# Splitting the two opening x loads of a mixture-of-experts kernel between two DMA issuers

## The chip, the cores and the metric

The kernel runs on one core of one Trainium2 chip. The metric is device time in microseconds (us), as the median of several runs. Before the change it is 181.49 us, the median of 3 runs that lie between 181.38 and 181.49.

## The reference

There are 8 experts. Each takes its own 256 tokens of 512 numbers through two matrix products with a ReLU between them. All data is float32 in the chip's main memory.

```python
n_experts, capacity, hidden, expert_hidden = 8, 256, 512, 2048
h = np.matmul(x, w1) + b1[:, np.newaxis, :]      # x [8,256,512], w1 [8,512,2048]
h = np.maximum(h, 0)
return np.matmul(h, w2) + b2[:, np.newaxis, :]   # w2 [8,2048,512]
```

The weights w1 and w2 are 4.2 MB each for each expert, 67 MB in all. They are used once, so the kernel is mostly a stream of loads.

## The kernel before, in words

The matrix products are done in float16. A DMA that GpSimd (POOL) issues changes float32 to float16 on its way, so w1 and w2 arrive in SBUF as float16, in `load_w1` (L84) and `load_w2` (L93). Each has three buffers. The x of experts 2 to 7 comes in the same manner, in two loads of several experts (`load_x`, L76). The x of the first two experts is the exception: it is loaded as float32 by SyncE (SP) at L190 into two tiles `x32`, each of 128 partitions with 2 token rows of 512 numbers (4096 bytes a partition, 512 KB a load), and VectorE (DVE) changes it to float16 at L201. The tiles come from `out_pool`, whose two buffers hold the results of experts 6 and 7 at the end.

Then x must be transposed, since TensorE (PE) contracts over partitions. DVE does this in 32x32 blocks: 16 instructions at L109 for each of the first two experts, 16 at L112 for each of the others. DVE also transposes the biases b1 into `b1T` with four instructions (L208).

`first_product(e)` runs 16 blocks of 4 matmuls (L121) into PSUM. After each block ScalarE (ACT) adds the bias, applies ReLU and writes float16 (L128). Its first activation therefore waits for `b1T`, and so does the activation-table load that stands ahead of it. `second_product(e)` runs 2 bias matmuls (L171) and 32 matmuls (L178); DVE and ACT copy the results out of PSUM (L156, L157). It trails the first product by `LAG = 3` experts.

Results of experts 0 to 3 and of 4 and 5 are gathered and stored by POOL (L140). Expert 6 is stored in three parts at L164: 25 rows by SP, 96 by ACT, 7 by SP. Expert 7 is stored by SP, in one part.

What sets the order: the instructions of PE and the DMAs of POOL are kept in program order by hand (`ordered`). The list `ring` says in which step each load is issued. A load into a weight buffer waits until the product that used it before is done. The other engines work through their own queues, in the order in which the program was written. In the opening, the program order is: the two x loads (SP), w1 of expert 0, b2, b1 rows (POOL), then the cast and transposes of expert 0, the cast and transposes of expert 1 (DVE; part of these come before and part after `b1T`), and the main loop, whose first step has w1 of expert 1, x of experts 2 and 3, and w1 of expert 2 on POOL.

The DMAs of SP go through one hardware queue (q1 in the profile), those of ACT through another (q10), and those of POOL through a software queue (q0). Before the change ACT issues one DMA in all, the 96 rows at L164.

Of the kernel before, what the change touches and what calls it, by code (L numbers as in the profile page):

```python
# [10 lines left out]
def kernel(  # L11
# [9 lines left out]
    nc = tc.nc  # L21
# [4 lines left out]
    P = 128  # L26
    nTB = T // P
# [54 lines left out]
    def load_w1(e):  # L82
        w1_sb[e] = w1_pool.tile([P, nKC, M], fp16, tag="w1", name="w1sb")
        ordered(nc.gpsimd.dma_start(  # L84
            out=w1_sb[e], in_=w1[e].rearrange("(p kc) m -> p kc m", kc=nKC)
        ))
# [100 lines left out]
    x32 = []  # L187
    for e in range(nXF32):
        x32.append(out_pool.tile([P, nTB, H], fp32, tag="out", name="x32"))
        nc.sync.dma_start(out=x32[e], in_=x[e].rearrange("(p tb) h -> p tb h", tb=nTB))  # L190
    load_w1(0)
    ordered(nc.gpsimd.dma_start(  # L192
        out=b2_sb,
        in_=b2.rearrange("e h -> (e h)").rearrange("(o f) -> o f", o=1),
# [12 lines left out]
    for b in range(nB):  # L207
        nc.vector.transpose(  # L208
            out=b1T[b * B : (b + 1) * B, nB - 1 - b : nB - 1 - b + nJ * B],
            in_=b1_rows.rearrange("r (i j) -> r j i", j=nJ),  # L210
# [55 lines left out]
```

## Time and profile before

| What | us |
|---|---|
| median of 3 runs | 181.49 |
| span of the profiled execution, first to last instruction | 179.7 |
| difference between the two | 1.8 |
| PE, DVE, ACT, POOL busy | 129.1, 88.0, 70.2, 13.1 |
| share of 16 DMA engines' span: q0, q1, q10 | 96.6%, 2.4%, 0.5% |
| read from and written to main memory | 71.39 MB, 4.19 MB |
| from issue to landing: the two x loads of L190 | 3.5 and 4.3 |
| granted TensorE clock, mean | 0.944 |

The profile is one execution, recorded by the hardware; the page does not give that execution's own whole time beside its span, so the runs' median stands there. Times in the views are counted from the first instruction. In a row of the timeline the first number is the start, the second the length, then engine, line, operation, what is written and read, and in brackets the idle time before it and what ended that. "SPq" and "ACTq" are rows of the issuing of a DMA; the transfer follows and is in the rows of the DMA queues. In the view of a stretch by slices, a digit is the busy share of the 16 DMA engines in tenths (9 is 90% or more).

### The profile page before, as it was taken

The numbers are of one execution on the slowest core, as the hardware profiler recorded it, in microseconds if no ns is written. First come the engines' busy times: TensorE is split into PE (matmuls) and PEld (weight loads), VectorE is DVE, ScalarE is ACT, GpSimd is POOL, SyncE is SP. The second block draws the span as 40 slices with busy tenths as digits, with TensorE's granted clock in tenths as the row PEclk, the third lists the DMA queues.
The fourth block names the chain that finished last, engine by engine and source line by source line (L and its number), as shares of the span: only waits on it lengthen the run. The fifth ranks groups of instructions, "written<-read, shape, count | busy, mean of one in ns | idle before, by whom it ended". The sixth has DMA issues, their size and how long they took to land.

```text
span 179.7 us, 1958 instructions
## 1 busy us (share of the span) xinstructions
PE 129.1 (72%) x784; PEld 85.8 (48%) x784; DVE 88.0 (49%) x125; ACT 70.2 (39%) x151; POOL 13.1 (7%) x28
## 2 busy tenths in 40 slices
PE   0005099969595970899969597969497887999950
PEld 0004079969592320795369244844195332433420
DVE  0999942987000199999999998003200020301010
ACT  0000459969593022483099005950586020020010
POOL 7000002120201010001010001000200021010000
PEclk9999999999998798589999889999999996999996
DMA  5999999999999999999999999999999999999996
GB/s 216 251 226 199 233 212 197 233 224 193 228 230 192 221 233 215 197 230 230 204 208 230 219 193 233 226 193 222 230 215 197 233 206 204 223 212 215 335 420 250
DMA packets 3829, 40.56 MB, mean 226 GB/s; under 512 B 461, under 2 KB 477, under 8 KB 1133
## 3 DMA queue, kind: packets, MB, share of 16 engines
q0 software_dynamic: 3232, 38.35, 96.6%
q1 hardware_dynamic: 476, 1.70, 2.4%
q10 hardware_dynamic: 112, 0.39, 0.5%
q8 instruction: 6, 0.10, 0.2%
q14 instruction: 3, 0.02, 0.0%
HBM read 71.39 MB, written 4.19 MB: 421 GB/s over the span
## 4 chain that ended last, share of the span: by engine, by line
DMA 66%; PE 26%; POOL 2%; another core or an unknown queue 1%; issue 1%; ACT 0%; POOLq 0%
DMA w1sb<-in_w_dram 44%; DMA w2sb<-in_w_dram 22%; PE po L178 18%; PE ph L121 8%; PE po L171 1%; POOL w1sb L84 1%; ACT out L157 0%; POOL x L76 0%; POOL b_sb L192 0%; POOL b_rows L196 0%; POOLq L250 0%
## 5 line engine op out<-in xcount | busy, mean ns | idle before, releaser
L121 PE MATMUL ph<-xT,w1sb 128*128 128x256 f16 x512 | 63.6, 289 | 34.8 <-DMA w1sb<-in_w_dram 23.9
L121 PEld LDWEIGHTS <-w1sb 128*128 128x128 f16 x512 | 59.0, 147 | 40.3 <-DMA w1sb<-in_w_dram 32.6
L178 PE MATMUL po<-w2sb,hT 128*128 128x512 f16 x256 | 61.4, 402 | 9.4 <-DMA w2sb<-in_w_dram 9.4
L112 DVE STREAM_TRANSPOSE xT<-x 32x256 f16<-32x256 f16 (+1 forms) x64 | 53.1, 889 | 25.6 <-DMA x<-in_x_dram 18.7
L128 ACT ACTIVATE hT<-ph,b1T 128x256 f16<-128x256 f32 x128 | 56.2, 474 | 13.6 <-PE ph L121 13.4
L178 PEld LDWEIGHTS <-hT 128*128 128x128 f16 x256 | 25.9, 102 | 44.7 <-issue 19.3
L156 DVE COPY out<-po 32x512 f32<-32x512 f32 (+2 forms) x22 | 15.1, 688 | 54.0 <-PE po L178 53.8
L157 ACT COPY out<-po 32x512 f32<-32x512 f32 (+2 forms) x22 | 12.7, 579 | 69.7 <-PE po L178 69.5
L109 DVE STREAM_TRANSPOSE xT<-x 32x256 f16<-32x256 f16 x32 | 14.0, 436 | 0.5
L93 POOL DMA_DIRECT2D w2sb<-in_w_dram x10 | 5.3, 534 | 72.8 <-PE po L178 72.8
L128 ACT ACT_TABLE_LOAD x1 | 1.3, 1283 | 20.5 <-DVE b1T L208 20.5
L84 POOL DMA_DIRECT2D w1sb<-in_w_dram x8 | 4.5, 558 | 63.2 <-PE ph L121 62.4
L171 PE MATMUL po<-b_sb,ones 1*128 1x512 f16 x16 | 4.8, 379 | 0.0
L208 DVE STREAM_TRANSPOSE b1T<-b_rows 32x512 f32<-32x512 f32 x4 | 4.1, 1035 | 0.1
L201 DVE CAST x<-x 128x1024 f16<-128x1024 f32 x2 | 1.5, 757 | 3.3 <-DMA x<-in_x_dram 3.3
L140 POOL DMA_DIRECT2D out_dram<-out x2 | 1.1, 542 | 10.9 <-ACT out L157 10.9
L171 PEld LDWEIGHTS <-ones 1*128 1x128 f16 x16 | 0.9, 92 | 2.1 <-issue 2.1
L76 POOL DMA_DIRECT2D x<-in_x_dram x2 | 1.1, 552 | 0.0
L197 DVE MEMSET ones<- 1x128 f16 x1 | 0.2, 165 | 0.8 <-PEq L250 0.8
L196 POOL DMA_DIRECT2D b_rows<-in_b_dram x1 | 0.5, 515 | 0.0
L192 POOL DMA_DIRECT2D b_sb<-in_b_dram x1 | 0.5, 513 | 0.0
L250 POOL MEMSET const-float32-0.0<- 128x1 f32 x1 | 0.1, 99 | 0.2 <-issue 0.2
(3 smaller groups left out, 0.3 us busy)
## 6 DMA issues: line engine op xcount, KB each, us to landing
w1sb<-in_w_dram POOLq DMA_DIRECT2D x8, 2048.0 KB, 34.5
w2sb<-in_w_dram POOLq DMA_DIRECT2D x6, 2048.0 KB, 46.8
w2sb<-in_w_dram POOLq DMA_DIRECT2D x4, 1024.0 KB, 24.0
out_dram<-out POOLq DMA_DIRECT2D x1, 2048.0 KB, 26.8
x<-in_x_dram SPq DMA_DIRECT2D x2, 512.0 KB, 3.9
x<-in_x_dram POOLq DMA_DIRECT2D x1, 1024.0 KB, 30.8
out_dram<-out POOLq DMA_DIRECT2D x1, 1024.0 KB, 17.8
x<-in_x_dram POOLq DMA_DIRECT2D x1, 512.0 KB, 24.0
```

The lines of the kernel that those rows point to most:

```text
L84: ordered(nc.gpsimd.dma_start(out=w1_sb[e], in_=w1[e].rearrange("(p kc) m -> p kc m", kc=nKC)))
L93: ordered(nc.gpsimd.dma_start(out=w2_sb[e][:, lo : lo + half], in_=src[:, lo : lo + half]))
L109: nc.vector.transpose(out=out[:, :, g, :, 0, :], in_=block[:, :, :, 0, :])
L112: nc.vector.transpose(out=out[:, tb, g], in_=block[:, tb])
L121: ordered(nc.tensor.matmul(out=ph, lhsT=w1_sb[e][:, kc, :].rearrange("p (q j) -> p q j", j=nJ)[:, :, j], rhs=xT[e][:, kc, :], start=(kc == 0),
L128: nc.scalar.activation(out=hT[e][:, j, :].rearrange("p (tb k i) -> p tb k i", tb=nTB, k=split), in_=ph.rearrange("p (tb i k) -> p tb k i", ...
L156: nc.vector.tensor_copy(out=out_sb[at : at + rows, k * nTB, :], in_=po[0][part])
L157: nc.scalar.copy(out=out_sb[at : at + rows, k * nTB + 1, :], in_=po[1][part])
L171: ordered(nc.tensor.matmul(out=t, lhsT=ones1, rhs=b2_sb[0:1, e * H : (e + 1) * H], start=True, stop=False,))
L178: ordered(nc.tensor.matmul(out=po[tb], lhsT=hT[e][:, j, tb * P : (tb + 1) * P], rhs=w2_sb[e][:, j, :], start=False, stop=(j == nJ - 1),))
L201: nc.vector.tensor_copy(out=t, in_=x32[e])
L208: nc.vector.transpose(out=b1T[b * B : (b + 1) * B, nB - 1 - b : nB - 1 - b + nJ * B], in_=b1_rows.rearrange("r (i j) -> r j i", j=nJ),)
```

## The change

Each of the two loads at L190 becomes two of 64 partitions: the lower half is issued by SP, the upper by ACT. Bytes, destination tiles and what reads them stay the same. As the program is built, ACT's two issues stand at the head of its queue, ahead of the table load; SP's two stand where its two stood; the cast of each tile waits for two landings in place of one, and so do ACT's last two copies, which write the tiles' buffers again. The order of the instructions on PE, DVE and POOL is the same. Lines below are shifted by two.

```diff
     for e in range(nXF32):
         x32.append(out_pool.tile([P, nTB, H], fp32, tag="out", name="x32"))
-        nc.sync.dma_start(out=x32[e], in_=x[e].rearrange("(p tb) h -> p tb h", tb=nTB))
+        src = x[e].rearrange("(p tb) h -> p tb h", tb=nTB)
+        nc.sync.dma_start(out=x32[e][: P // 2], in_=src[: P // 2])
+        nc.scalar.dma_start(out=x32[e][P // 2 :], in_=src[P // 2 :])
     load_w1(0)
```

## The prediction

> **What bounds the kernel now.** I read the page first (PE is busy 72% of the span, DMA shows 9 in every slice but the first and last), then the busy time by stages, the DMA view of the first 4 us, the timeline of the opening, and the chain of work that ended last. The stages come first. Columns: stage, its length, busy time of each engine with its count, the granted clock, the DMA share and GB/s.
>
> ```profile
> 0.00:2.00 2.00, 0.00 (x0) 0.00 (x0) 0.17 (x1) 0.00 (x0) 0.95 (x6) 1.00 0.10 27
> 2.00:4.60 2.60, 0.00 (x0) 0.00 (x0) 0.34 (x1) 0.00 (x0) 2.56 (x5) 1.00 1.03 383
> 4.60:15.30 10.70, 0.02 (x1) 0.03 (x1) 10.32 (x24) 0.00 (x0) 0.00 (x0) 1.00 1.05 227
> ...
> 149.50:158.20 8.70, 8.66 (x33) 3.46 (x33) 1.38 (x2) 0.00 (x0) 0.00 (x0) 0.81 1.02 214
> 158.20:173.40 15.20, 15.09 (x69) 6.25 (x68) 1.38 (x2) 1.81 (x4) 0.54 (x1) 1.00 1.02 289
> ...
> 177.00:179.70 2.70, 0.00 (x0) 0.00 (x0) 0.00 (x0) 0.00 (x0) 0.00 (x0) 0.50 0.35 143
> ```
>
> The DMA engines are full from 2 us to 177 us (share 1.02 to 1.05). They are the bound; PE works in pieces between landings. The chain that ended last says where DMA hands over:
>
> ```profile
> 110.12 39.38 DMA w2sb<-in_w_dram
> ...
> 149.54 8.66 PE po L178 x32
> ...
> 173.33 0.59 ACT out L157
> ```
>
> Until 149.5 us the path is loads, each queued behind the ones before; from there PE runs the last three second products without a wait, and ACT and the last store end the span. So the end moves with one thing: when the unbroken stream of DMA work begins, and how much work is in it. The change touches only its first 3 us. The DMA view of 0 to 4 us, in 40 slices of 0.1 us (busy tenths, then GB/s):
>
> ```profile
> DMA  0000000000000000056743299997998699999898
> GB/s 0 1 0 0 0 0 0 0 0 0 0 0 0 0 0 0 0 164 205 164 82 123 82 410 369 451 328 328 451 451 328 287 451 451 369 410 492 328 492 369
> ```
>
> The first x packet moves at 1.7 us, and for six slices the rate is 82 to 205 GB/s; then it is about 410. The six slices move 820 x 0.1 = 82 KB where full rate would move 246 KB: 164 KB, or 0.40 us of the stream, are lost in the start.
>
> **The change, part by part.** The opening, engine by engine:
>
> ```profile
> 0.74 0.87 SPq L190 DMA_DIRECT2D x<-in_x_dram  x2
> ...
> 4.26 0.82 DVE L201 CAST x<-x 128x1024 f16<-128x1024 f32 x1 [3.27 <-DMA x<-in_x_dram]
> ...
> 12.32 0.70 DVE L201 CAST x<-x 128x1024 f16<-128x1024 f32 x1
> ...
> 16.19 4.18 DVE L208 STREAM_TRANSPOSE b1T<-b_rows 32x512 f32<-32x512 f32 x4
> ...
> 20.45 1.28 ACT L128 ACT_TABLE_LOAD   x1 [20.45 <-DVE b1T L208]
> ...
> 22.28 7.89 PE L121 MATMUL ph<-xT,w1sb 128*128 128x256 f16 x52 [4.22 <-ACT hT L128]
> ```
>
> *Issues.* SP still issues two loads, of 64 rows. The row count hardly sets the price: L164's three issues on SP, of 25, 7 and 128 rows, took 0.36 to 0.60 us with the 128 rows (at 173.94) at 0.36; L190's took 0.40 and 0.42 for 128. So 0.36 to 0.60 each, and I take 0.40, the same kind of load. SP has nothing else until 166 us: 0. A first packet later by 0.60 - 0.40 = 0.2 us would be the upper end. ACT gets two issues, 2 x 0.38 (its L164 row) = 0.76 us, from about 0.74 to 1.5; behind them stands the table load, which starts at 20.45 because it waits for b1T: hidden with 18.9 us to spare. POOL's order is untouched.
>
> *The moved bytes.* The same 1 MB in the same rows of 4096 bytes. Two more loads add 32 packets of 4 bytes that mark a landing, two for each of 16 engines; even at the price of a data packet (next paragraph) that is 0.3 us, at the share of their bytes nothing. I take 0.02, nearest to their size.
>
> *The packets' own time.* In 1.5 to 4.5 us queue 1 used 85.3% of 16 x 3.0 us for 255 packets, 16 of them small: 40.9 / 239 = 171 ns for each 4096 bytes. ACT's final store, in 160 to 180 us, used 4.8% of 16 x 19.7 us for 96 data packets: 158 ns. Each DMA engine has 16 x packets, so x takes 2.7 us of every engine now, and 2.5 at best. With two queues feeding one engine the trace shows no row. Below: the start fills at once, -0.40 us (the loss above). Above: the packets of the ramp, where an engine moves 137 GB/s / 16 at a share of about 0.45 (the six slices' means), take 4096 / 19.0 = 215 ns; if all 16 stayed there, 16 x (215 - 171) = +0.70 us. I take -0.08, near the present row: the first descriptors still come 1.0 us after the same issue time, and the ramp is mostly a wait for the first data, which a second queue meets in the same microsecond.
>
> *The first landing.* x0 lands 3.5 us after its issue, at 4.2, and the cast at 4.26 waits for both halves after the change. If SP's half of x1 goes ahead of a late ACT half of x0, x0 is up to 4 packets, 4 x 171 ns = 0.7 us, later; at best 0.3 earlier (the filled ramp, less what x1 gains). Queued behind that cast on DVE are 16 transposes, the second cast and b1T, then ACT's table load and PE's first product: all move together. But none of it reaches the end:
>
> ```profile
> 38.62 7.21 PE L121 MATMUL ph<-xT,w1sb 128*128 128x256 f16 x64 [1.47 <-DMA w1sb<-in_w_dram]
> 47.66 7.21 PE L121 MATMUL ph<-xT,w1sb 128*128 128x256 f16 x64 [1.84 <-DMA w1sb<-in_w_dram]
> ```
>
> After its first two products PE stands 1.47 us before the third expert's w1, and 1.84 us before the fourth's. A late start of up to 1.47 us is gone there. Its other outlet is the load that POOL issues at 30.46 once the first product is done. The loads queued before it last until 38.57 (4.00 + 34.57 in the chain), and from issue to first packet w1 took at most 3.3 us (1.25 to about 4.6, the end of the x packets), so 38.57 - 30.46 - 3.3 = 4.8 us remain. An early start buys nothing for the same reason. Cost: 0, if x0 is less than 1.47 us late. x1 lands at 1.2 + 4.3 = 5.5 and is cast at 12.32: 6.8 us of cover.
>
> *Late waits.* ACT's two last copies and SP's final list wait for four x landings in place of two, all 160 us old: two waits of 17 ns (L164's row) and before PE's end or the last landing. 0 to 0.03; I take 0.
>
> [...]
>
> **The sum.** 0.02 - 0.08 + 0 = -0.06 us on a span of 179.7. The runs show 181.49 (181.38 to 181.49), 1.8 more than the profiled span, and that remainder is untouched: 181.49 - 0.06, about **181.4**. A measurement of this kernel can tell about 0.2%, 0.36 us, from no change.
>
> **The rivals.**
> *The start fills (faster).* Two queues bring requests to the engines sooner, and the ramp of 0.40 us goes; a first packet earlier by the 0.06 us that an issue may shorten (0.42 to 0.36) adds to it. For it: the slices at 82 GB/s, which look like one queue waiting for data. Against: w1's first packet must be ready when x is done, and the trace shows none before 4.5 us, so its own latency may cap the gain. Price -0.36 to -0.46: 181.0.
> *Two queues hinder each other (slower).* At the engines, packets of both halves alternate between rows 64 apart, and each takes longer. Price up to +0.70 us (+0.90 with the slowest issue), all of it at the end since the stream has no hole until 177 us: 182.1. It leaves the 0.2% band from 0.36 / 16 = 22 ns a packet. Against it: packets that meet w1's stream and the stores in the last 20 us still show 158 ns.
> *The clock in the tail.* The product at 149.54 took 8.66 us, its successors about 7.1, at clocks of 0.81 and 1.00; one slow stretch costs 1.6 us there. A shift could add one: 183.1. Or remove it: then PE is ahead of the last w2 and only about 0.5 us come back, 181.0. [...] Three runs within 0.11 us speak against such jumps.
> *The split does nothing at all* is inside the forecast: the halves share all engines.
>
> **How the numbers follow.** Forecast 0.54 (181.13 to 181.85); start fills 0.20; queues hinder 0.15; tail clock slower 0.08, faster 0.03. Faster by over 0.2%: 0.20 + 0.03 = 0.23; slower: 0.15 + 0.08 = 0.23; within: 0.54. The range, 180.8 to 182.3, takes in the bounds -0.46 and +0.70 (+0.90 but for 0.1) with the spread of the runs, and leaves out most of the tail's slow case.
>
> **What would show it.** Right: two queues of 128 data packets each in the first 5 us, the first packet at about 1.7, the first cast within 0.7 us of 4.26, PE idle for about 1.5 us before the third expert's product, and the last w2 wait ending within 0.3 us of 149.5. Wrong: the six slow slices gone and every landing earlier by 0.4 (start fills); a q1 and q10 mean well over 171 ns and every landing later (hinder); a product of the last three at a clock other than now (tail); or a hole in the DMA row behind 4.6 us, which I hold to be out.

## The result and the profile after

The divided loads take 182.22 us (median of 11 runs, 181.99 to 182.68) where the kernel before took 181.53 beside them (11 runs, 181.38 to 182.04). The ratio is 1.0033, with a 95% interval of 1.0025 to 1.0042: about 0.6 us slower. The profiled execution is the slowest of the eleven (182.68, span 180.9), so its times are somewhat later than those of a median run would be.

The stages of the opening, in the columns used above:

```profile
0.00:2.00 2.00, 0.00 (x0) 0.00 (x0) 0.17 (x1) 0.00 (x0) 0.95 (x6) 1.00 0.00 0
2.00:4.60 2.60, 0.00 (x0) 0.00 (x0) 0.00 (x0) 0.00 (x0) 2.56 (x5) 1.00 1.12 258
4.60:15.30 10.70, 0.00 (x0) 0.00 (x0) 9.26 (x21) 0.00 (x0) 0.00 (x0) 1.00 1.04 241
```

The DMA engines look as full as before from 2 to 4.6 us (share 1.12 against 1.03) but move 258 GB/s in place of 383. A share says that a packet is under way, not how fast it goes. The first 4 us in slices of 0.1 us:

```profile
DMA  0000000000000000000049998078759999799599
GB/s 0 0 0 0 0 0 0 0 0 0 0 0 0 0 0 0 0 0 0 0 164 246 451 164 287 0 328 164 205 246 328 410 287 287 164 369 205 123 819 656
```

The first packet is at 2.0 to 2.1 us, not at 1.7, and the rate stays mostly at 160 to 330 GB/s where it had been about 410. (The last two slices hold the start of w1's large packets.) The timeline shows the issues and what waits for them:

```profile
0.74 1.18 SPq L191 DMA_DIRECT2D x<-in_x_dram  x2
0.74 1.45 ACTq L192 DMA_DIRECT2D x<-in_x_dram  x2
...
5.67 0.69 DVE L203 CAST x<-x 128x1024 f16<-128x1024 f32 x1 [4.68 <-DMA x<-in_x_dram]
...
13.64 0.69 DVE L203 CAST x<-x 128x1024 f16<-128x1024 f32 x1
...
16.38 2.78 PE L121 MATMUL ph<-xT,w1sb 128*128 128x256 f16 x12 [16.38 <-DMA w1sb<-in_w_dram]
```

SP's two issues take 1.18 us together (0.55 and 0.58) where they took 0.87. The first cast is 1.41 us later, and PE can start on w1 of expert 0 at 16.38, against 15.28 before. What follows from each, on PE:

```profile
29.76 16.32 PE L121 MATMUL ph<-xT,w1sb 128*128 128x256 f16 x148
48.40 8.88 PE L121 MATMUL ph<-xT,w1sb 128*128 128x256 f16 x64 [2.31 <-DMA w1sb<-in_w_dram]
...
150.57 7.07 PE L178 MATMUL po<-w2sb,hT 128*128 128x512 f16 x32 [0.38 <-DMA w2sb<-in_w_dram]
...
170.22 3.61 PE L178 MATMUL po<-w2sb,hT 128*128 128x512 f16 x16 [0.95 <-DMA w2sb<-in_w_dram]
```

The late cast is swallowed, as the working had it: the 1.47 us that PE stood before the third product are gone, and the fourth product still waits for its load. The late stream is not swallowed: the w2 that ended the last long wait lands at 150.52, 1.02 us later than before. Here the slow stretch of the clock fell elsewhere (granted clock 1.00 from 149.5 to 158.2 us, 0.81 before), and PE, at 7.07 us a product, then had to wait 0.95 us for the last half of w2. ACT's last copy starts 0.54 us later than before (173.87 against 173.33), but the span ends 1.2 us later. The rest lies in the stores, which share the late stream: from 174 us on, POOL's queue still moves 1.29 MB, where it moved 0.97 before.

### The profile page after: what moved, and what is told of

Read it like the earlier page. It is cut to its first block, busy times and chain, and to the rows that moved or that the text cites. A ratio compares the mean times of both kernels' runs of the same rounds, so it can differ in the third digit from the quotient of the medians.

```text
span 180.9 us, 1963 instructions
## 1 busy us (share of the span) xinstructions
PE 129.1 (71%) x784; PEld 86.4 (48%) x784; DVE 87.8 (49%) x125; ACT 70.3 (39%) x151; POOL 13.0 (7%) x28
## 3 DMA queue, kind: packets, MB, share of 16 engines
q1 hardware_dynamic: 348, 1.18, 1.9%
## 4 chain that ended last, share of the span: by engine, by line
DMA 43%; PE 40%; DVE 4%; another core or an unknown queue 4%; ACT 3%; issue 1%; ACTq 0%; POOL 0%
DMA w1sb<-in_w_dram 25%; PE ph L121 24%; PE po L178 16%; DMA w2sb<-in_w_dram 11%; DMA x<-in_x_dram 7%; DVE b1T L210 2%; DVE xT L109 2%; ACT out L157 2%; PE po L171 1%; ACT L128 1%; ACT hT L128 1%; DVE x L203 0%; ACTq L192 0%; POOL w2sb L93 0%
## 5 line engine op out<-in xcount | busy, mean ns | idle before, releaser
L121 PE MATMUL ph<-xT,w1sb 128*128 128x256 f16 x512 | 65.0, 294 | 37.8 <-DMA w1sb<-in_w_dram 25.2
L121 PEld LDWEIGHTS <-w1sb 128*128 128x128 f16 x512 | 60.0, 147 | 43.6 <-DMA w1sb<-in_w_dram 35.1
L178 PE MATMUL po<-w2sb,hT 128*128 128x512 f16 x256 | 60.0, 394 | 7.0 <-DMA w2sb<-in_w_dram 7.0
```

Of the source, the lines that this page charges most:

```text
L121: ordered(nc.tensor.matmul(out=ph, lhsT=w1_sb[e][:, kc, :].rearrange("p (q j) -> p q j", j=nJ)[:, :, j], rhs=xT[e][:, kc, :], start=(kc == 0),
L178: ordered(nc.tensor.matmul(out=po[tb], lhsT=hT[e][:, j, tb * P : (tb + 1) * P], rhs=w2_sb[e][:, j, :], start=False, stop=(j == nJ - 1),))
```

## The experiments

All ratios are against the kernel before, run beside it on the same chip. The edits are shown shortened; `src` is x[e] in the form in which the kernel loads it. "First packet" and the landings are from the packet and landing records of the trace; a packet's mean time is worked out as in the prediction, share x stretch x 16 / data packets.

### First four: is it the halves, the two issuers, or ScalarE?

```diff
 e1:  SP  x32[e][: P // 2], then SP  x32[e][P // 2 :]      # for e = 0, 1
 e2:  SP  x32[0] whole, ACT x32[1] whole
 e3:  ACT x32[0] whole, ACT x32[1] whole
 e4:  as e2, and ahead of ACT's load
+        nc.scalar.activation(out=x32[e][:1, 0, :1], in_=ones1[:1, :1], func=Relu, scale=1.0)
```

(In e4 `ones1` is also set earlier, since the activation reads it.)

> All four halves of 64 rows issued by SyncE alone, one after the other; ScalarE issues none. Theory A (two hardware queues that issue in the same microsecond hold each other up, so the first x packets come late and the whole stream of loads with them): no second issuer, so SP's issues take about 0.4 us as before, the first x packet is at 1.7 to 1.8 us, the time is that of before, 181.5 (ratio 0.999 to 1.001). Theory B (loads of 64 rows are the cost, whoever issues them): 182.2 as with the change, ratio 1.003. Theory C (ScalarE's queue is slow to start): 181.5. Theory D (packets of two queues alternate on a DMA engine and each takes longer): 181.5, one queue.

> No halves: x of expert 0 whole by SyncE, x of expert 1 whole by ScalarE, both at once. Theory A: as with the change, SP's issue takes 0.5 to 0.6 us, its first packet is at about 2.06 us and ScalarE's later, time 182.0 to 182.3 (ratio 1.002 to 1.004). Theory B: 181.5. Theory C: SP's x0 is untouched, first packet 1.77, ScalarE's first packet about 1 us after it, which x0's packets cover: 181.5 to 181.8. Theory D: first packet at 1.77 us, but a mean well over 171 ns a packet where both queues run, 182.2.

> Both whole loads issued by ScalarE alone, none by SyncE. Theory A: one issuer, so the issues take about 0.4 us, the first packet is at 1.7 to 1.8 us, 181.5 (ratio 0.999 to 1.001). Theory B and theory D: 181.5. Theory C: the first packet at about 2.7 us as ScalarE's was with the change, the stream about 1 us later, 182.3 to 182.6.

> As the run with x0 whole by SyncE and x1 whole by ScalarE, but ScalarE first loads its activation table and runs one activation of a single element, so that its issue comes 1.3 to 1.6 us after SyncE's. Theory A: the issues don't meet, SP's takes 0.4 us, its first packet is at 1.7 to 1.8, and x1's packets (first at about 3.3) come as x0's end: 181.4 to 181.7. Theory B: 181.5. Theory C: ScalarE's first packet a full 2 us after its issue, about 4.3 us, by when w1's packets fill the engines: 181.5 to 181.7. Theory D: x1 now alternates with w1's packets and not with x0's, 181.5 to 182.

| Run | median us | ratio, interval |
|---|---|---|
| e1 halves, SP alone | 184.07 (182.34 to 184.57) | 1.0107 (1.0062 to 1.0152) |
| e2 whole, SP and ACT at once | 181.69 | 0.9988 (0.9970 to 1.0005) |
| e3 whole, ACT alone | 181.84 | 1.0006 (0.9982 to 1.0030) |
| e4 whole, ACT 1.5 us later | 184.44 | 1.0132 (1.0099 to 1.0164) |

My own first theory, A, falls with e2. Two issuers in the same microsecond, undivided, don't hold each other up:

```profile
0.74 0.39 SPq L191 DMA_DIRECT2D x<-in_x_dram  x1
0.74 0.41 ACTq L191 DMA_DIRECT2D x<-in_x_dram  x1
```

Its first packet is at 1.76, and in 2 to 5 us ACT's queue, with SP's beside it, takes 161 ns for each of its 128 data packets (43.0% of 48 us; columns: packets with the small ones, MB, share):

```profile
q10 hardware_dynamic: 138, 0.52, 43.0%
```

That takes theory D, the rival of the prediction, with it: two queues at once cost no time here. C falls with e3. What stays is the halves: e1, with one issuer, issues each in 0.55 to 0.60 us and sends its first packet at 2.08.

But e1 and e4 lose much more than B said. Their rows show why. The timeline of e1, VectorE first and then GpSimd, and last VectorE of e4:

```profile
10.90 0.69 DVE L203 CAST x<-x 128x1024 f16<-128x1024 f32 x1 [9.91 <-DMA x<-in_x_dram]
```

```profile
35.00 0.53 POOL L84 DMA_DIRECT2D w1sb<-in_w_dram  x1 [30.44 <-PE ph L121]
```

```profile
17.91 0.69 DVE L206 CAST x<-x 128x1024 f16<-128x1024 f32 x1 [5.85 <-DMA x<-in_x_dram]
```

In e1 the second half of x0 is issued at 1.34 and lands at 10.8. The packets of w1, issued by POOL at 1.25, start first, at 3.2 us; from 4.5 us on, a data packet of x (172 ns) goes by turns with one of w1 (1.23 us). In e3 the second load, issued by ACT at 1.15, is through by 5.0 us. So here a load that was issued 0.09 us after w1 (e1) fell behind it. With x0 6.6 us late, the POOL issue at 30.46 moves to 35.00, close to the edge that the prediction puts at 35.3 (38.57 - 3.3). In e4 it is x1 that falls behind; w1's landings spread over 3.1 us across the 16 engines where before they spread over 0.5, with single w1 packets of 2.3 and 2.4 us.

e4 also goes past the edge: there POOL issues at 35.49, and around 37 us twelve weight packets take 1.7 to 2.2 us in place of 1.23. In 36 to 38 us e4 moves 139 GB/s, e1 238. The row of e4, in the columns of the stages:

```profile
36.00:38.00 2.00, 2.00 (x21) 2.00 (x20) 1.96 (x6) 2.00 (x6) 1.07 (x3) 1.00 0.94 139
```

Averaged over the 16 engines, the landings behind it are about 1.1 us later than in the kernel before, those ahead of it 0.2 to 0.5. So a POOL issue that is too late does cost the stream. What makes the long packets near 3 and 5 us, and what separates e1's two runs near 182.3 (one of them the profiled one) from its four near 184.3, stays open.

### Next four: where the time of the halves goes

```diff
 f2:  SP x32[e][:, 0], ACT x32[e][:, 1]                    # 128 partitions, one token row each
 f6:  ACT x32[e][: P // 2], SP x32[e][P // 2 :]
 f5:  the change, with load_w1(0) moved behind the loads of b2_sb and b1_rows
 f3:  the kernel before, and ahead of SP's loads, for both tiles
+        nc.vector.memset(x32[e][:1, 0, :P], 0.0)
```

> Halves again, one by SyncE and one by ScalarE at once, but cut the other way: each load has all 128 partitions and one of the two token rows, 2048 bytes a partition. Theory R (a load of 64 partitions takes longer to issue, 0.55 us in place of 0.40, and starts late): the issues take about 0.40 us, the first packet is at 1.7 to 1.8 us, x is through before w1's packets, 181.5 to 181.9 (ratio 0.999 to 1.002). Theory P (16 engines that write into only the upper 64 partitions slow each other to about 300 ns a packet): the same, all partitions are written. Theory Q (whatever ScalarE's queue carries beside SyncE's is served slowly): ScalarE's packets slow again, 182.2. Theory W (x packets whose issue comes after w1's take turns with w1's packets, and that spreads the engines): as R, if the second pair is issued by 1.2 us.

> The change with the engines swapped: ScalarE loads partitions 0 to 63, SyncE 64 to 127. Theory P: the slow packets of about 300 ns in 2.8 to 4.5 us move to SyncE's queue, with the upper half. Theory Q: they stay with ScalarE's queue. Time by either, by R and by W: 182.2 (ratio 1.002 to 1.005).

> The change, with the two small bias loads issued by GpSimd ahead of w1 of expert 0 and not behind it, so that w1 is issued about 1.0 us later and the x rows don't share the engines with it. Theory W: the spread of w1's landings over the engines falls from 1.0 to about 0.5 us and most of the loss goes, 181.6 to 181.9 (ratio 1.000 to 1.002). Theories R, P and Q: the first packet still at 2.06, the slow packets still there, 182.1 to 182.3 (ratio 1.002 to 1.005).

> The kernel before, undivided, but VectorE first writes 128 numbers into each x tile (the load overwrites them), so that SyncE's loads are issued about 0.3 us later, as late as the divided ones send their first packet. If the lateness of the first packet is what the end shows, one for one: first packet at about 2.06, 181.8 to 181.9 (ratio 1.001 to 1.002). If a late first packet costs nothing: 181.5. If the second load now comes behind w1 and takes turns with it (theory W): x of expert 1 lands far later than 5.5 us, and the time is 182 or more.

| Run | median us | ratio, interval |
|---|---|---|
| f2 halves by token row | 181.61 | 0.9989 (0.9969 to 1.0008) |
| f6 swapped | 182.19 | 1.0031 (1.0014 to 1.0048) |
| f5 biases first | 183.13 | 1.0075 (1.0048 to 1.0103) |
| f3 SP 0.28 us later | 182.16 | 1.0017 (0.9999 to 1.0036) |

f2 is the change without its fault: divided between two engines, but with all 128 partitions in each part. The issues take 0.39 to 0.46 us, x is through at 5.2, and the time is that of before. So neither dividing nor the second engine costs anything here (ratio 0.9989); dividing the partitions does (the change, 1.0033).

f6 against the change tells where the slow packets sit. The queue of ACT in 2 to 5 us, first in the change, then in f6:

```profile
q10 hardware_dynamic: 80, 0.26, 38.4%
```

```profile
q10 hardware_dynamic: 80, 0.26, 37.4%
```

That is 18.4 / 64 = 288 ns and 18.0 / 64 = 280 ns a packet, whether ACT loads the upper or the lower half. So P, the upper half as such, falls. Q, which expected this outcome, had fallen with f2, where ACT's packets of 2048 bytes take 85 ns beside SP's. Of the first load's packets, SP's, half or more go at about 160 ns in both; but its landing is late. In the kernel before, an engine's landing of the first load follows its last packet by 0.33 to 0.37 us. With a contiguous half first it is 0.8 to 0.9 us (e1: packets through at 3.21 to 3.54, landed at 4.08 to 4.43). What fills that time no record shows.

f5 takes w1 out of the way, and theory W as the main cost falls: the time gets worse, not better. Columns: packets, MB, share, in 2 to 7 us:

```profile
q10 hardware_dynamic: 160, 0.52, 46.1%
q1 hardware_dynamic: 160, 0.52, 41.9%
```

With nothing between them the half loads are slow, 288 ns a packet on ACT's queue and 262 on SP's; the first of the four, on SP's, shows it in its landing alone, 0.8 to 0.9 us after its packets. They land at 4.1, 5.3, 6.5 and 7.7 us, one after the other, 262 KB in 1.2 us: about 220 GB/s. In the change, w1's packets come between the halves; whether they make up for part of the lost rate no run shows.

f3 comes nearest to a late start alone: the undivided loads go out 0.28 us later, the first packet is at 2.05, and the time is 0.3 us longer by the ratio, with an interval that just reaches zero.

```profile
1.02 0.87 SPq L192 DMA_DIRECT2D x<-in_x_dram  x2
```

In its profiled run the landings, each averaged over the 16 engines, are later than before by 0.21 to 0.25 us up to 159 us, so the stream passes the delay on. The line of theory W came true as well: its second load, issued at 1.47, falls behind w1 and lands at 11.4, and the median is 182.16. That the stream is late by the 0.25 us of the start alone speaks against a further cost of the turns there.

### Next four: partitions that lie apart, a control, and each part alone

```diff
 f7:  SP x32[e][0::2], ACT x32[e][1::2]
 f5b: the kernel before, with load_w1(0) moved as in f5
 f10: x32[0] whole by SP; x32[1] halved as in the change
 f11: x32[0] halved as in the change; x32[1] whole by SP
```

> 64 partitions a load again, one load by SyncE and one by ScalarE, but every other partition (0, 2, 4 ... and 1, 3, 5 ...), so that each load reaches over all 128. Theory P2 (while all 16 DMA engines write into one contiguous half of the partitions, lower or upper, they get only about 220 GB/s together, 250 to 300 ns a packet): packets of 160 to 180 ns here, and only the late first packet is left, 181.8 to 182.0 (ratio 1.001 to 1.002). Theory S (any load of 64 partitions has slow packets): 250 to 300 ns, 182.2 (ratio 1.003). By both the issue takes about 0.55 us if the count of partitions sets it; if it goes by where they lie, 0.40 and 181.6.

> Control: the kernel before, undivided, with the two small bias loads ahead of w1 of expert 0 as in the run of the change with the biases first. If w1's later issue is the cost there: 182.5 or more. If it is x at half rate (theory P2): x is through at about 5.1 us, w1 is ready by then, 181.5 to 181.8.

> x of expert 0 whole by SyncE, x of expert 1 halved, one half by each engine. Theories P2 and S with the late start: SP's first packet is at 1.76 again, only ScalarE's half (issued in 0.55 us) and SP's second issue are of 64 partitions; 181.6 to 181.9 (ratio 1.000 to 1.0015). If the mere use of both engines costs the time: 182.2.

> x of expert 0 halved, one half by each engine, x of expert 1 whole by SyncE behind its half. The first packet at 2.06 as with the change and slow packets for the second half served; x of expert 1 takes turns with w1. If the first load's lateness and its half rate are the loss: nearly all of it, 182.0 to 182.2 (ratio 1.002 to 1.003). If the second pair of halves is: 181.6 to 181.8.

| Run | median us | ratio, interval |
|---|---|---|
| f7 every other partition | 182.49 (181.83 to 183.14) | 1.0046 (1.0028 to 1.0064) |
| f5b control | 181.67 | 1.0002 (0.9993 to 1.0011) |
| f10 only x1 halved | 182.24 | 1.0038 (1.0020 to 1.0056) |
| f11 only x0 halved | 182.45 | 1.0055 (1.0031 to 1.0080) |

The control holds: w1's place costs nothing by itself (181.67), so f5's loss is that of the halves: x at about half the rate (220 GB/s, where the kernel before ran at about 410), and the late start. f7 gives ACT's packets back their speed: 25.1% of 48 us in 2 to 5 us, 188 ns a packet, most of them at 159. The issue is still 0.53 to 0.57, so that does not go with where the partitions lie. Its time, though, is a miss for my theory: 182.49 is no better than the change. f10 is a miss as well: with x0 whole and the first packet at 1.76 I expected 181.6 to 181.9, and x1's halves alone cost 0.7 us. Their packets are slow (305 ns a packet in SP's half, 210 in ACT's), and SP's half also falls behind w1 in part: its last packet ends at 9.5 us. f11, with only x0 halved, loses 1.0 us, more than either line of its expectation. So each pair of halves is enough for a loss like the whole change's. The parts don't add up.

### Last three: the two costs, each without the other

```diff
 g0:  the change
 g1:  f7 again
 g2:  SP x32[e][:96], ACT x32[e][96:]
```

> The change itself, on the same chip as the next run. Ratio 1.003 to 1.0045, first packet at about 2.06 us, ScalarE's packets at about 300 ns.

> Every other partition, on the same chip. If the half rate is a real part of the loss (b): 0.2 to 0.3 us below the change, ratio 1.0015 to 1.0025. If lateness alone (a) is what the time shows: the same as the change, 1.003 to 1.0045.

> SyncE loads 96 partitions, ScalarE 32. If the issue is long for any count but 128: both about 0.55 us, first packet about 2.06, 182.0 to 182.4. If it goes by the count (fewer, longer): 96 at about 0.45, 32 at 0.6 or more. If it is long at 64 alone: 0.40 for both, first packet at 1.77, 181.5 to 181.8. By (b) ScalarE's 32 partitions also lie in the upper half: packets of 250 ns and more.

| Run | median us | ratio, interval | first packet | x, us of each engine |
|---|---|---|---|---|
| g0 the change | 182.10 | 1.0017 (1.0003 to 1.0032) | 2.06 | 3.47 |
| g1 every other | 182.12 | 1.0016 (0.9997 to 1.0036) | 2.06 | 2.92 |
| g2 96 and 32 | 182.02 | 1.0017 (1.0006 to 1.0028) | 1.75 | 3.51 |

The last column is the time of all x data packets of queues 1 and 10, divided by 16; it is 2.72 in the kernel before. It is no price in itself, for it holds the wait of the first packets too: e2 has 3.15 and f2 2.98 without a loss. ACT's queue in 2 to 5 us, in g0 and then in g1:

```profile
q10 hardware_dynamic: 80, 0.26, 38.7%
```

```profile
q10 hardware_dynamic: 80, 0.26, 22.3%
```

That is 290 and 167 ns a packet: one contiguous half is slow, every other partition is not. The two kernels differ in nothing else. The first load's landing agrees: 0.9 us behind its packets in g0, 0.36 in g1. And g2's issues, then its two queues in 2 to 5 us:

```profile
0.74 0.85 SPq L191 DMA_DIRECT2D x<-in_x_dram  x2
```

```profile
q1 hardware_dynamic: 177, 0.66, 74.4%
q10 hardware_dynamic: 80, 0.25, 26.9%
```

Two issues in 0.85 us, with ACT's two in 0.89: 96 and 32 partitions go out like 128. The packets take 223 ns on SP's queue and 212 on ACT's, slow but not the 250 that I had named. The time is a miss too: with short issues I expected 181.5 to 181.8. Nor is 64 the whole rule of the issue: in f11 SP's second issue, a whole load of 128 partitions behind a half, took 0.57.

So g2 has the slow packets without the late start, g1 the late start without the slow packets, and g0 both. But g1 has one thing more, which g0 shares and g2 does not: its second loads fall behind w1 and take turns with it until 11.7 us. All three come out 0.3 us slower, with intervals that overlap. So slow packets alone are enough for a loss of this size (g2). What g1 has seems to be enough as well: its own interval just reaches zero, that of the same kernel in f7 does not.

What the causes cost together is not settled by the medians. The change itself measured 1.0033 in the first comparison and 1.0017 here, every other partition 1.0046 in f7 and 1.0016 here. The profiled runs show it more finely. There the landing of the second w1, averaged over the engines, is at 24.80 in the kernel before, 25.28 in g2, 25.31 in g1 and 25.59 in g0; and up to 160 us the later landings stay behind those of the kernel before by the same 0.5, 0.5 and 0.8 us, to about 0.1 (0.25 in f3, 0.1 in e2). So g0 does lose 0.3 us more of the stream than either. Of g1's 0.5, f3 accounts for 0.25 by the same late first packet; what the other half is stays open, and the turns with w1 are a candidate.

No run points to a version that beats the kernel before: e2 and f2 equal it.

## Why the prediction was wrong

The forecast was no change, 181.4, from a sum of -0.06 us. The time rose by 0.33%, about 0.6 us, past the 0.2% band. It stayed inside the range of 180.8 to 182.3 and came close to the rival "two queues hinder each other", 182.1, which had 0.15; but the reason that this rival gives is not what the runs show (below).

**What bounds the kernel** was right: the stream of loads has no hole, and what delays its start is carried to the end (f3: 0.28 us of delay, 0.25 us in the landings, about 0.3 us of time).

**The issues**: here is the first failed step. "The row count hardly sets the price", I wrote, from L164's stores and L190's loads of 128 rows, and took 0.40 of a bound of 0.36 to 0.60. A load of 64 partitions takes 0.55 (e1, g0). The first packet comes 0.29 us later: more than the 0.15 that the issue grew by, and more than the 0.2 that I had as the upper end. The rows I went by held no load of 64, and g2 shows that I could not have got it by drawing a line through the counts: 32 and 96 are at 0.39 to 0.45. Why 64 is dear no run tells.

**The packets' own time**: the second failed step, and the larger in the profile. I took -0.08 within -0.40 to +0.70, because the row before stood at 171 ns. The change has 3.50 us of x on each engine in place of 2.72: +0.78 us, just above the upper bound, whose 215 ns a packet met the measured 219. The bound was about right, by luck, since it came from the packets of the ramp; the reason for staying near the present row was not right: I argued from queues and never asked where the packets write. (Not all of the 0.78 is price, as e2 shows; the stream of the change is 0.8 to 0.9 us later in all, the late start included.) By the rival's own words packets alternate "between rows 64 apart"; that is not it, since f5's halves land one after the other, 1.2 us apart, and are slow all the same, while whole loads on two queues (e2) run at 161 ns. What goes with the slow packets is that a load lies in one contiguous half of the partitions (f5's 288 and 262 ns against f5b's 166, which is 80.6% of 51.2 us for 248 data packets; g0's 290 against g1's 167). f5 also has a rate for such a half: 262 KB in 1.2 us, about 220 GB/s. What makes it slow no run shows.

**The first landing**: the price of 0 held, with 0.06 us to spare, and that was luck. The cast came 1.41 us later; 1.47 was the allowance, and PE's pause before the third product vanished, while the fourth still waited for its load. I gave 0.7 as the most for this delay, which was too little. The further edge, 35.3, agrees with the runs: e1's issue at 35.00 left no gap in the stream, e4's at 35.49 did.

**x1's cover of 6.8 us** was used up to the last: the second cast came at 13.64, just after its halves had landed (13.6), since the second issues now fall behind w1 and take turns with it. I had no step for that. The late cast cost nothing here; e1 and e4, where loads fell far behind w1 too, lost about 2 us.

**The tail** behaved as its rival said: at full clock, PE came up against the last w2, and the gain was 0.5 us. The three runs within 0.11 us, on which I played jumps down, were few: beside the experiments the kernel before ranges from 181.38 to 183.16.

## What to carry to other kernels

If a load has to be divided at all, divide it along its free dimension and not across the partitions: f2 cost nothing, the halves 0.2 to 0.3%, every other partition 0.16 and 0.46% in two comparisons, 96 and 32 0.17%. When a view says that DMA engines are full, read the GB/s beside it before calling them busy (from 2 to 4.6 us, a share of 1.12 went with 258 GB/s after the change, one of 1.03 with 383 before). Where a cost is bounded from both sides by distant rows, ask which resource the new operation uses differently (here, where it writes) before going with the nearest row.

## What was not expected of the hardware

A load of 64 partitions took 0.53 to 0.60 us to issue, on SP and on ACT, contiguous or every other (ACT's second beside SP's second 0.84); loads of 32, 96 and 128 took 0.38 to 0.46, but for one of 128 that stood behind a half and took 0.57 (f11). In these runs 0.14 to 0.27 us in the time of issue decided much: an undivided load that SP issued at 1.20 went whole ahead of w1, issued by POOL at 1.25, while a half issued at 1.34 (e1) and a whole load issued at 1.47 (f3) took turns with it, one x packet of 172 ns for each of 1.23 us, and landed at 10.8 us (x of expert 0, 4.2 before) and 11.4 (x of expert 1, 5.5 before).
